# Value product of a hybrid attention trunk: the second read of one weight block is loaded with the first six tiles

## The chip, the cores and the metric

The kernel runs on one core of a Trainium2 chip. The metric is device time in microseconds of one execution. Three runs of the kernel before took 1443.1, 1443.45 and 1443.83 us (median 1443.45). One further execution was recorded by the hardware profiler and took 1444.35 us; all profile rows come from it, with times counted from the start of its span.

## The reference, cut to what matters

One layer over 1024 tokens of width 1024, in float32: an input projection gives queries, keys and values for 8 heads of a banded softmax attention (A) and 8 heads of a stick-breaking attention (B), and two gates; both branches are projected, gated, summed and projected again; LayerNorm, a SwiGLU feed-forward, LayerNorm.

```python
h = x @ w_in[l]
qa, ka, va, qb, kb, vb, ga, gb = jnp.split(h, split_pts, axis=-1)
y_a = chunk_band_attention(heads_a(qa), heads_a(ka), heads_a(va), rel_bias[l]) @ w_proj_a[l]
y_b = stick_breaking_attention(heads_b(qb), heads_b(kb), heads_b(vb)) @ w_proj_b[l]
mix = (sigmoid(ga + b_gate[l, :D]) * y_a + sigmoid(gb + b_gate[l, D:]) * y_b) @ w_out[l]
x = layer_norm(DEEPNORM_ALPHA * x + mix, ln1_g[l], ln1_b[l])
```

The change lies in the part of `x @ w_in` that gives `va` and `vb`: the value product, 1024 x 1024 times 1024 x 1024.

## The kernel before

**Arithmetic.** Every float32 operand is split into a high part, rounded on ScalarE (L110), and a low part, the difference, made on VectorE (L111); one product of a pair costs three matmuls (high by high, high by low, low by high). Large products are done by a seven-product scheme on 2 x 2 blocks (Strassen's, in Winograd's form): sums of blocks are formed on VectorE, seven block products p run in the order 1, 2, 6, 5, 7, 3, 4, and their results are added into four quarters. For the value product the weights are four blocks of 512 x 512, each held as two tiles of 128 x 1024 (halves h = 0, 1). X is block 0, U is block 3, Z is block 2, and block 1 is here called Y.

**Stages.** The input projection goes by pairs of column tiles: `plain` (pair 0), then pairs 1 to 4 (q and k), then the value product (`v`, `V_AT = 5`), pairs 6 to 8 (q and k) and five pairs of gates. Each pair has products named sxp, syp, szp; the tile `wcp4` is the third right operand of pair 4, read by its product 3 (szp<-s24h,wcp). Then come the attention heads one after the other (scores `sc_a`, transposes `tp_a`, value products `pv_a`, with gate matmuls `gps` mixed in as fill), the merge, and the FFN.

**The value product.** `v_load` (L413) runs while pair 4 computes; it asks for two tiles each of X, U and Z and issues their loads (L420). `v_prepare(p)` (L422) makes the operands of product p, while the product before it runs. For p = 1, 2, 5, 3, 4 it splits X, Z, X, U, Z as they stand at that time. For p = 6 it loads Y (L432) and forms, in place, X <- Y - X (L434), Y <- U - X (L435), Z <- Z - Y (L436), and splits the new Y. For p = 7 it loads block 1 again and takes U minus it (L438). High and low parts are `vh6`, `vl6` and so on, named by product. A product has 48 matmuls of 128 x 512 (2 halves, 4 rows of output j, 2 by 3 operands); products 1, 6, 7, 4 add up in one set of four PSUM banks, 2 in a second set, which 5 and 3 take over. After product 1 ScalarE copies the four banks out (`vc`, L489); after product 2 VectorE adds its banks on (L491), the sums are split and stored (L459).

**What sets the order.** All loads and stores go through SP's queue in the order in which the scheduler put them; a waiting one holds up those behind it. SBUF tiles come from rings of named buffers: `gt` has 3, `kp` 4, `op` 8; a new tile takes the buffer of the oldest tile of its tag and waits for that one's last reader. `cycle(QKV, ...)` goes round the four tags qs, kh, kl, v of two buffers each, so that eight tiles fill it once; stores of the pairs, outputs of the value product, gate tiles and later merged and FFN tiles all turn this ring, and the attention takes head tiles `qs`, `kh`, `kl`, `v` of the same buffers directly. The scheduler also decides the order on each engine from what it believes to be ready.

Of the kernel before, what the change touches and what calls it, by code (L numbers as in the profile page):

```python
# [48 lines left out]
def hybrid_trunk_kernel(ctx: ExitStack, tc, x, xt, w_first, w_v, w_in, b_gate, rel_bias, w_proj,  # L49
# [14 lines left out]
    def slot(tag, name, dtype=F32):  # L64
        return pool.tile([P, 1024], dtype, tag=tag, name=name, bufs=SLOTS[tag])
# [3 lines left out]
    def cycle(tags, name, dtype=F32):  # L69

        turn_of[tags] = turn_of.get(tags, -1) + 1
        return slot(tags[turn_of[tags] % len(tags)], name, dtype)

    QKV = ("qs", "kh", "kl", "v")
# [9 lines left out]
    dma = nc.sync.dma_start  # L84
# [24 lines left out]
    def split(dst_h, dst_l, src):  # L109
        return (nc.scalar.copy(dst_h, src),  # L110
                nc.vector.tensor_tensor(dst_l, src, dst_h.bitcast(F32), ALU.subtract))  # L111
# [298 lines left out]
    v_src = [[None] * 2 for _ in range(3)]  # L410
    v_ops = {}

    def v_load():  # L413

        for n, (blk, tags) in enumerate(((0, ("gt", "gt")), (3, ("gt", "kp")), (2, ("kp", "kp")))):
            for h, tag in enumerate(tags):
                v_src[n][h] = slot(tag, f"wv{blk}_{h}")
        for n, blk in ((0, 0), (2, 2), (1, 3)):
            for h in range(2):
                dma(v_src[n][h], w_v[blk, h])  # L420

    def v_prepare(p):  # L422

        put, sub = nc.vector.tensor_tensor, ALU.subtract
        v_ops[p] = []
        for h in range(2):
            X, U, Z = (v_src[n][h] for n in range(3))
            hi, lo = (slot("op", f"v{s}{p}_{h}", F32R) for s in "hl")
            src = {1: X, 2: Z, 5: X, 3: U, 4: Z}.get(p)
            if src is None:  # L430
                src = cycle(QKV, f"wv1_{p}{h}") if p == 6 else slot("gt", f"wv1_{p}{h}")
                dma(src, w_v[1, h])  # L432
                if p == 6:
                    put(X, src, X, sub)  # L434
                    put(src, U, X, sub)  # L435
                    put(Z, Z, src, sub)  # L436
                else:
                    put(src, U, src, sub)  # L438
            split(hi, lo, src)
            v_ops[p].append((hi, lo))  # L440

    def v_steps():
# [18 lines left out]
        def step(p, following):  # L461
# [3 lines left out]
            def run():  # L465
                if following:
                    v_prepare(following)
                if first:
                    for j in range(4):
                        tag = ("mm", "mm", "sc", "sc")[j] if accs is by else ("tr", "tr", "tr", "pv")[j]  # L470
                        accs[j] = bank(tag, f"v{p}_{j}")
                for h in range(2):
                    for j in range(4):
                        for i in range(2):
                            kt = 2 * h + i
                            xh_, xl_ = (x[:, j * P:(j + 1) * P] for x in ops_x[p][kt])
                            wh, wl = (w[:, (LO, HI)[i]] for w in v_ops[p][h])
                            for n, (a, b) in enumerate(((xh_, wh), (xh_, wl), (xl_, wh))):
                                mm(accs[j], a, b, start=(first and kt == n == 0),  # L479
                                   stop=(kt == 3 and n == 2), skip_group_check=True)  # L480
                for j in range(4):
                    acc = spread(accs[j])
                    if p == 4:
                        done("21", j, acc)
                        continue
                    name = {1: "11", 2: "11", 6: "12", 3: "12", 5: "22", 7: "22"}[p]
                    raw = tile_of(name, j)[1]
                    if p in (1, 6, 5):
                        nc.scalar.copy(raw, acc)  # L489
                    else:  # L490
                        nc.vector.tensor_tensor(raw, acc, raw, ALU.add)  # L491
                        done(name, j, raw)
# [134 lines left out]
    def right_or_v(i):  # L627
        if i + 1 == V_AT:
            v_load()
            v_prepare(1)  # L630
        else:
            right(i + 1)
# [794 lines left out]
```

## Time and profile before

| what | us |
|---|---|
| median of three runs | 1443.45 |
| profiled execution | 1444.35 |
| its span, first to last instruction | 1442.6 |
| busy: PE / VectorE / ScalarE / GpSimd | 1421.1 / 1028.6 / 673.0 / 267.8 |
| value product, first to last start on PE | 94.8 to 194.4 |
| attention heads | about 347 to 640 |

PE is the matmul engine, PEld its weight loads, DVE VectorE, ACT ScalarE, POOL GpSimd, SP the queue that issues the DMAs (SPq). A timeline row gives start, duration, engine, line, operation, out<-in, and in brackets the idle time of the engine before it with what ended it. A row of waits reads: who waited <- for whom: total, times, longest.

### The profile page before, as it was taken

How to read it: one execution, taken by the hardware profiler on the slowest of the kernel's cores; microseconds unless marked ns; L12 is line 12 of the kernel's file. 1: busy time of each engine (PE TensorE's matmuls, PEld its weight loads, DVE VectorE, ACT ScalarE, POOL GpSimd, SP SyncE). 2: the span in 40 equal slices, each digit the busy share in tenths (PEclk: the TensorE clock that was granted, in tenths of full speed). 3: DMA queues.
4: the chain of work that ended last, by engine and by line, in shares of the span. 5: the costliest groups of instructions: out<-in, count | busy, mean ns of one | idle time of the engine just before them, and what ended most of it. 6: DMA issues, size and time to landing. Idle time of an engine off the chain costs nothing.

```text
span 1442.6 us, 19078 instructions
## 1 busy us (share of the span) xinstructions
PE 1421.1 (99%) x6696; PEld 1178.6 (82%) x6696; DVE 1028.6 (71%) x1638; ACT 673.0 (47%) x1171; POOL 267.8 (19%) x317
## 2 busy tenths in 40 slices
PE   9997999999999999999999999999999999999997
PEld 7785888888888888888888888888888888888886
DVE  8856565654777878887858966676777755978757
ACT  6443444555787888773313634444444433221201
POOL 0000000001555778850014000000000000100016
PEclk9998999999999999999999999999999999999999
DMA  7565357868677587867512123434444457786602
GB/s 248 149 203 165 127 205 220 283 205 251 195 214 193 166 239 239 270 197 274 178 37 95 55 106 127 143 143 157 161 160 146 150 201 260 287 306 240 204 15 103
DMA packets 102544, 263.99 MB, mean 183 GB/s; under 512 B 11040, under 2 KB 27424, under 8 KB 102448
## 3 DMA queue, kind: packets, MB, share of 16 engines
q1 hardware_dynamic: 102448, 262.77, 55.5%
q8 instruction: 53, 0.87, 0.3%
q14 instruction: 43, 0.35, 0.1%
HBM read 170.94 MB, written 88.11 MB: 180 GB/s over the span
## 4 chain that ended last, share of the span: by engine, by line
PE 93%; DVE 3%; ACT 1%; DMA 1%; issue 1%; POOL 0%; SPq 0%; POOLq 0%; DVEq 0%; ACTq 0%
PE sxf L180 16%; PE sxp L180 8%; PE szf L180 8%; PE dx L1350 6%; PE v L479 5%; PE gps L573 4%; PE szp L180 4%; PE syf L180 4%; PE dz L1350 3%; PE yAps L870 3%; PE syp L180 2%; PE tp_b L781 2%; PE tp_a L781 2%; PE ops L118 2%; PE ops L117 2%; PE ops L120 2%
## 5 line engine op out<-in xcount | busy, mean ns | idle before, releaser
L1306 POOL TENSOR_TENSOR wdyt<-wdyt 128x512 f32<-128x512 f32 x8 | 11.1, 1394 | 512.3 <-ACT h L1178 422.6
L758 POOL TENSOR_TENSOR w_b<-w_b,kp_b 128x511 f32<-128x511 f32 (+3 forms) x96 | 96.4, 1015 | 31.8 <-DVE kp_b L753 22.5
L753 DVE TENSOR_TENSOR_SCAN kp_b<-kp_b,ident_ps 128x512 f32<-128x512 f32 (+2 forms) x64 | 56.6, 885 | 23.3 <-ACT kp_b L750 22.4
L750 ACT ACTIVATE kp_b<-sc_b 128x512 f32<-128x512 f32 (+3 forms) x96 | 48.4, 504 | 30.7 <-PE sc_b L670 25.4
L1058 POOL TENSOR_TENSOR mv<-mv,neghalf 128x1 f32<-128x1 f32 x16 | 23.9, 1494 | 207.6 <-DVE mv L1057 207.6
L693 POOL MEMSET bias<- 64x64 f32 x2 | 0.3, 145 | 327.3 <-ACT bias L689 327.3
L180 PE MATMUL szf<-x1S63h,wcf 128*128 128x512 f32 x168 | 55.1, 389 | 0.0
L111 DVE TENSOR_TENSOR pt_b<-tp_b,pt_b 128x512 fp32r<-128x512 f32 (+1 forms) x96 | 50.0, 544 | 6.8 <-ACT pt_b L110 6.2
L1281 DVE TENSOR_TENSOR x<-dx,x 128x512 f32<-128x512 f32 x64 | 43.5, 687 | 14.9 <-PE dx L1350 14.9
L723 POOL TENSOR_SCALAR w_a<-w_a,st_a 128x640 f32<-128x640 f32 (+2 forms) x64 | 42.4, 667 | 61.6 <-PE sc_a L670 26.5
L111 DVE TENSOR_TENSOR sl<-h,sl 128x512 fp32r<-128x512 f32 x56 | 38.5, 687 | 20.1 <-ACT sl L110 20.1
L110 ACT CAST sl<-h 128x512 fp32r<-128x512 f32 x56 | 34.7, 619 | 36.2 <-PE syf L180 17.1
L110 ACT CAST pt_b<-tp_b 128x512 fp32r<-128x512 f32 (+1 forms) x96 | 47.5, 505 | 8.0 <-PE tp_b L781 7.6
L718 ACT ACTIVATE w_a<-w_a,st_a 128x640 f32<-128x640 f32 (+2 forms) x64 | 44.8, 700 | 12.4 <-DVE st_a L712 11.2
L118 PE MATMUL ops<-wl_o,mh 128*128 128x512 f32 x128 | 50.1, 392 | 0.0
L120 PE MATMUL ops<-wh_o,ml 128*128 128x512 f32 x128 | 49.9, 390 | 0.0
L117 PE MATMUL ops<-wh_o,mh 128*128 128x512 f32 x128 | 49.7, 391 | 0.0
L1178 ACT ACTIVATE h<-sxf 128x512 f32<-128x512 f32 x21 | 12.6, 598 | 77.7 <-PE sxf L180 77.7
L751 ACT ACTIVATE w_b<-sc_b 128x511 f32<-128x511 f32 (+3 forms) x96 | 48.6, 506 | 0.0
L781 PE MATMUL tp_b<-ident,w_b 128*128 128x128 f32 x288 | 47.8, 273 | 0.4 <-DVE pt_b L111 0.3
L111 DVE TENSOR_TENSOR pt_a<-tp_a,pt_a 128x512 fp32r<-128x512 f32 (+1 forms) x96 | 44.8, 485 | 4.6 <-ACT pt_a L110 3.1
L110 ACT CAST pt_a<-tp_a 128x512 fp32r<-128x512 f32 (+1 forms) x96 | 39.1, 432 | 11.0 <-PE tp_a L781 10.7
(1740 smaller groups left out, 4784.8 us busy)
## 6 DMA issues: line engine op xcount, KB each, us to landing
s_dr<-sl SPq DMA_DIRECT2D x112, 256.0 KB, 2.3
sd<-s_dr SPq DMA_DIRECT2D x56, 512.0 KB, 4.8
wLf<-in_w_ffn_in_dram SPq DMA_DIRECT2D x22, 512.0 KB, 4.5
wRf<-in_w_ffn_in_dram SPq DMA_DIRECT2D x22, 512.0 KB, 3.5
v_dr<-vc SPq DMA_DIRECT2D x16, 512.0 KB, 3.0
kh<-k_dr SPq DMA_DIRECT2D x32, 256.0 KB, 5.8
kl<-k_dr SPq DMA_DIRECT2D x32, 256.0 KB, 6.0
qs<-q_dr SPq DMA_DIRECT2D x16, 512.0 KB, 5.5
```

The costliest lines, as they stand in the source:

```text
L110: return (nc.scalar.copy(dst_h, src), nc.vector.tensor_tensor(dst_l, src, dst_h.bitcast(F32), ALU.subtract))
L111: nc.vector.tensor_tensor(dst_l, src, dst_h.bitcast(F32), ALU.subtract))
L117: mm(acc, lh, rh, start=(i == 0), stop=False)
L118: mm(acc, lh, rl, start=False, stop=False)
L120: mm(acc, ll, rh, start=False, stop=(i == n))
L180: mm(acc, lw[:, ks], rx, start=(first and kt == i == 0), stop=(kt == 3 and i == 2), skip_group_check=not first)
L479: mm(accs[j], a, b, start=(first and kt == n == 0), stop=(kt == 3 and n == 2), skip_group_check=True)
L573: mm(acc[hf], lw[:, ks], rx[k][:, (LO, HI)[hf]], start=(k == j == 0), stop=(k == KT - 1 and j == 2))
L753: nc.vector.tensor_tensor_scan(kp[:, 0:e], kp[:, 0:e], ident_ps()[:, 0:e], 0.0, ALU.mult, ALU.add)
L758: nc.gpsimd.tensor_tensor(be[:, m0:e], be[:, m0:e], kp[:, m0 - 1:e - 1], ALU.mult)
L781: tr(tp[:, (qb - lo_q) * P:(qb - lo_q + 1) * P], wt[qb - q0][:, (kb - qb) * P:(kb - qb + 1) * P], ident)
L1350: mm(acc, a, b, start=(first and i == n == 0), stop=(i == n - 1 == 1), skip_group_check=not first)
```

## The change

Y's two tiles are asked for in `v_load`, one as the fourth `kp` tile, one from the QKV ring, and their loads are issued there, behind those of X, Z and U. `v_prepare(6)` takes these tiles; before, both were taken from the ring, and loaded, in `v_prepare(6)`. The second copy of block 1 for product 7 is loaded as before. Lines from L418 on move by up to four.

```diff
                 v_src[n][h] = slot(tag, f"wv{blk}_{h}")
+        again = [slot("kp", "wv1_60"), cycle(QKV, "wv1_61")]
         for n, blk in ((0, 0), (2, 2), (1, 3)):
             for h in range(2):
                 dma(v_src[n][h], w_v[blk, h])
+        for h in range(2):
+            dma(again[h], w_v[1, h])
+        v_src.append(again)
...
-            X, U, Z = (v_src[n][h] for n in range(3))
+            X, U, Z, Y = (v_src[n][h] for n in range(4))
             hi, lo = (slot("op", f"v{s}{p}_{h}", F32R) for s in "hl")
             src = {1: X, 2: Z, 5: X, 3: U, 4: Z}.get(p)
             if src is None:
-                src = cycle(QKV, f"wv1_{p}{h}") if p == 6 else slot("gt", f"wv1_{p}{h}")
-                dma(src, w_v[1, h])
+                src = Y if p == 6 else slot("gt", f"wv1_{p}{h}")
                 if p == 6:
                     put(X, src, X, sub)
                     put(src, U, X, sub)
                     put(Z, Z, src, sub)
                 else:
+                    dma(src, w_v[1, h])
                     put(src, U, src, sub)
```

The instructions are the same in number; their order moves. In SP's queue, in the value product (`wv2_1` and `wv3_1` are half 1 of Z and U, `wv1_60` and `wv1_61` the halves of Y, `k_dr4` and `q_dr4` the stores of pair 4, `vc11` the first output), before:

```order
L336 DMA q_dr4_81<-c1_4_959 64x1024
L432 DMA wv1_61_1155<-in_w_v_dram 128x1024
L459 DMA v_dr0_93<-vc11_0_1136 128x1024
L432 DMA wv1_60_1146<-in_w_v_dram 128x1024
L459 DMA v_dr0_93<-vc11_1_1138 128x1024
```

and now:

```order
L421 DMA wv2_1_966<-in_w_v_dram 128x1024
L421 DMA wv3_1_964<-in_w_v_dram 128x1024
L423 DMA wv1_60_967<-in_w_v_dram 128x1024
L423 DMA wv1_61_968<-in_w_v_dram 128x1024
L335 DMA k_dr4_89<-hi2_4_1053 64x1024
```

The two loads of Y moved ahead of the eight stores of pair 4 and of the stores of `vc11`; no other load changed its place there. On PE, product 3 of pair 4 (12 matmuls) moved from behind 4 matmuls of v to behind 22.

On VectorE, in product 2 (`wv0` X, `wv3` U, `wv2` Z), from the last work of pair 4 on, before:

```order
L389 SCALAR_TENSOR_TENSOR c1_4_959<-c1_4_959,hi1_4_1069 128x1024
L491 TENSOR_TENSOR vc11_0_1136<-v2_0_1162,vc11_0_1136 128x8x64
L491 TENSOR_TENSOR vc11_1_1138<-v2_1_1163,vc11_1_1138 128x8x64
L111 TENSOR_TENSOR vc11_0_1136<-vc11_0_1136 128x8x64
L491 TENSOR_TENSOR vc11_2_1140<-v2_2_1164,vc11_2_1140 128x8x64
L111 TENSOR_TENSOR vc11_1_1138<-vc11_1_1138 128x8x64
L491 TENSOR_TENSOR vc11_3_1142<-v2_3_1165,vc11_3_1142 128x8x64
L111 TENSOR_TENSOR vc11_2_1140<-vc11_2_1140 128x8x64
L111 TENSOR_TENSOR vc11_3_1142<-vc11_3_1142 128x8x64
L434 TENSOR_TENSOR wv0_1_962<-wv1_61_1155,wv0_1_962 128x1024
L435 TENSOR_TENSOR wv1_61_1155<-wv3_1_964,wv0_1_962 128x1024
L436 TENSOR_TENSOR wv2_1_966<-wv2_1_966,wv1_61_1155 128x1024
```

and now:

```order
L389 SCALAR_TENSOR_TENSOR c1_4_959<-c1_4_959,hi1_4_1073 128x1024
L437 TENSOR_TENSOR wv0_0_961<-wv1_60_967,wv0_0_961 128x1024
L438 TENSOR_TENSOR wv1_60_967<-wv3_0_963,wv0_0_961 128x1024
L437 TENSOR_TENSOR wv0_1_962<-wv1_61_968,wv0_1_962 128x1024
L439 TENSOR_TENSOR wv2_0_965<-wv2_0_965,wv1_60_967 128x1024
L111 TENSOR_TENSOR vl6_0_1149<-wv1_60_967,vh6_0_1148 128x1024
L438 TENSOR_TENSOR wv1_61_968<-wv3_1_964,wv0_1_962 128x1024
L495 TENSOR_TENSOR vc11_0_1140<-v2_0_1162,vc11_0_1140 128x8x64
L439 TENSOR_TENSOR wv2_1_966<-wv2_1_966,wv1_61_968 128x1024
L111 TENSOR_TENSOR vl6_1_1156<-wv1_61_968,vh6_1_1155 128x1024
L111 TENSOR_TENSOR vc11_0_1140<-vc11_0_1140 128x8x64
L495 TENSOR_TENSOR vc11_1_1142<-v2_1_1163,vc11_1_1142 128x8x64
```

The sums of Y stood behind all eight `vc11` instructions and now stand ahead of them, with one addition between. On ScalarE at the same place, now:

```order
L110 CAST vh6_0_1148<-wv1_60_967 128x1024
L110 CAST vh6_1_1155<-wv1_61_968 128x1024
L110 CAST vc11_0_1140<-vc11_0_1140 128x8x64
L110 CAST vh5_0_1230<-wv0_0_961 128x1024
L110 CAST vc11_1_1142<-vc11_1_1142 128x8x64
L110 CAST vh5_1_1234<-wv0_1_962 128x1024
L493 COPY vc11_3_1146<-v1_3_1091 128x8x64
```

Before, the copy of the fourth bank (`vc11_3<-v1_3`) stood ahead of the first cast of `vc11` and of all casts of `vh6`. On PE the product's fourth bank is now first written after 19 matmuls, the first product with half 1 one place ahead of it.

At the start of the attention, on SP (`qs1`, `kl1`, `v1` belong to head 1, `c1_13` and `c2_13` are the last gate tiles), before:

```order
L397 DMA g_dr8_111<-c1_13_2582 128x1024
L535 DMA wr_g11_2780<-in_w_in_dram 128x1024
L650 DMA qs1_2692<-q_dr0_77 128x1024
L663 DMA v1_2861<-v_dr0_93 128x8x128
L650 DMA qs2_2927<-q_dr1_78 128x1024
```

and now:

```order
L397 DMA g_dr8_111<-c1_13_2582 128x1024
L539 DMA wr_g11_2780<-in_w_in_dram 128x1024
L667 DMA v1_2861<-v_dr0_93 128x8x128
L657 DMA kl1_2697<-k_dr0_85 64x1024 x2
L654 DMA qs2_2927<-q_dr1_78 128x1024
```

Head 1's `kl` changed places with its `qs`, which now goes out earlier; a few of head 0's and head 1's matmuls on PE moved by some places with them. Behind the first three heads the order is again the same.

## The prediction

> **What bounds the kernel now.** I read the page first: the span and the engines' busy times.
>
> ```profile
> span 1442.6 us, 19078 instructions
> PE 1421.1 (99%) x6696; PEld 1178.6 (82%) x6696; DVE 1028.6 (71%) x1638; ACT 673.0 (47%) x1171; POOL 267.8 (19%) x317
> ```
>
> TensorE works 1421.1 of 1442.6 us. A change that adds and removes no matmul can win only where TensorE waits, or where its clock is cut. So the second view is the list of waits of PE, and the third the busy time and clock in stretches around the value product.
>
> ```profile
> PE v L479 <- ACT vh L110: 9.3, 1, 9.3
> PE warm L267 <- DVE warm L264: 1.2, 1, 1.2
> 120.00:130.00 10.00, 8.10 (x36) 6.38 (x34) 5.06 (x8) 2.48 (x4) 0.00 (x0) 1.00 0.77 203
> 130.00:140.00 10.00, 2.62 (x6) 1.94 (x7) 9.86 (x10) 3.72 (x4) 0.00 (x0) 0.65 0.48 190
> 140.00:150.00 10.00, 10.00 (x38) 8.04 (x38) 5.64 (x5) 2.40 (x4) 0.00 (x0) 0.84 0.32 105
> ```
>
> (After the stretch come its length and the busy times of PE, PEld, DVE, ACT, POOL, then the clock, DMA share and GB/s.) One wait of 9.3 us stands in the value product; the next in size is 1.2 us at the start. Around it the granted clock falls to 0.65 and 0.84, so the stall costs twice: idle, and then slow matmuls. The timeline of PE prices both.
>
> ```profile
> 127.71 0.39 PE L479 MATMUL v<-vh,xl 128*128 128x512 f32 x1
> 137.38 1.65 PE L479 MATMUL v<-vh,s24h 128*128 128x512 f32 x3 [9.28 <-ACT vh L110]
> ...
> 142.71 0.63 PE L479 MATMUL v<-vh,s24l 128*128 128x512 f32 x1
> 143.13 0.45 PE L479 MATMUL v<-vl,s24h 128*128 128x512 f32 x1
> ...
> 150.91 0.39 PE L479 MATMUL v<-vh,s24l 128*128 128x512 f32 x1
> 151.14 0.39 PE L479 MATMUL v<-vh,s13h 128*128 128x512 f32 x1
> ```
>
> A warm 128x512 matmul follows the one before after 0.227 us (150.91 to 151.14 is 0.23; product 5 runs like that throughout). Product 2 ends with the matmul at 127.71, so product 6 could start at 127.94; it starts at 137.38: 9.44 us. Its 48 matmuls last to 151.14, 13.76 us, where 48 x 0.227 is 10.88: 2.88 us more, all of it before 143.4, where starts lie 0.43 us apart. Together 12.32 us.
>
> What is late? Product 6 needs the tiles `vh6`, `vl6`, made by VectorE (L434 to L436) and ScalarE (L110) from Y, the block 1 that L432 loads.
>
> ```profile
> 120.31 0.62 SPq L336 DMA_DIRECT2D q_dr<-c  x1
> 121.04 1.01 SPq L432 DMA_DIRECT2D wv<-in_w_v_dram  x1
> 126.73 0.33 SPq L459 DMA_DIRECT2D v_dr<-vc  x1
> 127.18 0.37 SPq L432 DMA_DIRECT2D wv<-in_w_v_dram  x1
> DMA to landing us min/median/max: 3.5/4.6/5.7
> 117.92 1.22 DVE L389 SCALAR_TENSOR_TENSOR c<-c,hi 128x1024 f32<-128x1024 f32 x1
> 124.06 0.69 DVE L491 TENSOR_TENSOR vc<-v,vc 128x512 f32<-128x512 f32 x1 [4.92 <-PE v L479]
> 130.12 1.22 DVE L434 TENSOR_TENSOR wv<-wv,wv 128x1024 f32<-128x1024 f32 x1
> 131.37 1.23 DVE L435 TENSOR_TENSOR wv<-wv,wv 128x1024 f32<-128x1024 f32 x1
> 132.63 1.22 DVE L436 TENSOR_TENSOR wv<-wv,wv 128x1024 f32<-128x1024 f32 x1
> 133.77 1.22 DVE L434 TENSOR_TENSOR wv<-wv,wv 128x1024 f32<-128x1024 f32 x1
> 136.28 3.89 ACT L110 CAST vh<-wv 128x1024 fp32r<-128x1024 f32 x4 [6.81 <-DVE wv L435]
> ```
>
> Y is asked for in product 2 only: half 1 at 121.04, half 0 at 127.18, behind the first `vc` store, which waits for product 2's result. (`DMA to landing` is the time from issue to landing of all loads of block tiles, the group `wv`.) VectorE is idle for 4.92 us before 124.06, then clears the eight `vc` instructions and only then forms the six sums, 130.12 to 137.5. The first split ends at 137.3 and PE starts.
>
> **The change part by part.** It issues no instruction more or less: the two loads of Y move on SP from behind pair 4's stores to behind U's, and every tile of the QKV ring that follows takes a neighbouring buffer.
>
> *When Y lands.* On SP the six loads end so:
>
> ```profile
> 102.63 1.56 SPq L420 DMA_DIRECT2D wv<-in_w_v_dram  x2
> 113.19 0.45 SPq L335 DMA_DIRECT2D k_dr<-hi  x1
> 94.75 0.39 PE L479 MATMUL v<-vh,xh 128*128 128x512 f32 x1
> 95.66 0.43 PE L180 MATMUL szp<-s24h,wcp 128*128 128x512 f32 x1
> ```
>
> SP is free at 104.2. Y's half 0 takes the `kp` buffer of `wcp4`, which product 3 of pair 4 reads (szp<-s24h,wcp). Before, that starts at 95.66, after four matmuls of v; in the new order 22 stand ahead: 94.75 + 22 x 0.227 = 99.7, and with its own 12 it ends near 102.9. So no wait at 104.2; were there one, the queue behind holds pair 4's stores, which have nothing to send before 113.19: 9 us of cover. With 4.6 us (5.7 at most) to land, both halves are there by 110 to 111.
>
> *When product 6 is ready.* VectorE now takes the sums right behind L389 at 117.92. Starts lie 1.25 us apart where one reads the other's result (130.12, 131.37) and 1.14 where not (132.63, 133.77); a `vc` sum is 0.60. In the new order: X0 119.06, Y0 120.31, X1 121.45, Z0 122.59, vl6_0 123.73, Y1 124.87, vc_0 126.01 (its bank is ready, at 124.06 before), Z1 126.61, vl6_1 127.74, done 128.96. PE wants the first half at 127.94 and `vl6_1` after 25 matmuls, at 133.6: 3.0 us to spare on the first (vl6_0 is done at 124.95) and 4.6 us on the second. The 9.44 us go, and with them the idle time ahead of the slow matmuls, 2.88.
>
> *What is late next.* ScalarE's copy of the fourth bank out of product 1 (vc_3) has moved behind casts that follow VectorE's sums, and product 6 may not write that bank before it.
>
> ```profile
> 124.78 0.62 ACT L110 CAST vc<-vc 128x512 fp32r<-128x512 f32 x1 [6.11 <-DVE vc L491]
> 111.60 0.59 ACT L489 COPY vc<-v 128x512 f32<-128x512 f32 x1 [3.37 <-PE v L479]
> ```
>
> VectorE: low part of vc_0 at 128.88, sum vc_1 at 129.48, ended 130.17; ScalarE: cast vc_1 0.62, cast vh5_1 1.05, copy 0.59 with 0.1 overlap each, ending near 132.25. PE asks for the bank after 19 matmuls: 127.94 + 4.31 = 132.25. No slack. From below 0, from above one more 1.2 us VectorE instruction in the chain; I take 0.2, since every term is a measured one and the ends meet.
>
> *Products 5 and 7.* v5 is needed at 138.8 (127.94 + 10.88), its halves follow with five more instructions of VectorE each, near 132 and 135; v7's loads go out behind the last `vc` store, near 136, and land near 141: with one sum, one cast and one low part (1.23 + 1.05 + 1.22) near 145 for product 7 at 149.7. Nothing is taken for either.
>
> *The ring's turn.* Y now advances the ring once instead of twice, so every tile after the product sits one buffer further back. At the start of the attention one tile is worse off by it: head 1's `kl`. Its buffer is now that of a last gate tile, and its load stands on SP behind that tile's store and behind head 1's v.
>
> ```profile
> 345.18 2.94 SPq L397 DMA_DIRECT2D g_dr<-c  x2
> 348.69 0.73 SPq L650 DMA_DIRECT2D qs<-q_dr  x1
> 350.73 0.54 SPq L663 DMA_DIRECT2D v<-v_dr  x1
> 355.69 0.30 PE L670 MATMUL sc_a<-kl,qs 128*128 128x320 f32 x1
> 358.88 0.60 PE L781 MATMUL tp_a<-ident,w_a 128*128 128x128 f32 x4
> DMA to landing us min/median/max: 4.9/6.2/9.2
> ```
>
> (The last row is `kl` in 330 to 380 us.) On the clock of before, the second half of kl1 goes out at 351.9 and lands at 358.1, at worst 361.1. Its first reader was at 355.69. In the new order 7 gate, 4 value, 7 transpose matmuls and one of scores stand between the first scores with kh1 (near 355.3) and it: 12 x 0.227 or a little less, and 7 x 0.11 (four transposes take 0.60, the last one's 0.27 included), about 3.3 us, so near 358.6. Cost 0 to 2.5 us. The median landing leaves nothing, so I take a small 0.4.
>
> *Sum.* 12.3 - 0.2 - 0.4 = 11.7 us. The profiled execution took 1444.35 us (span 1442.6 and 1.75 around it): 1432.65. The median of the runs lies 0.9 below that execution, so **1431.8 us**.
>
> A rule on the slow matmuls: in the trace starts stay 0.43 us apart for 6.0 us after the stall (137.38 to 143.4), which cost 2.88. The Trainium skill (TensorE: Matmul & The Clock Gate, Part 1: The HAM clock gate) says that an idle window of some 3.4 us halves the clock and about 3.4 us of activity restores it; by that the slow matmuls cost half of 3.4, an estimate of 1.7 us, and the time would be 1433.0. The trace agrees on the half rate, not on the length; I go by the trace.
>
> **The rivals.** *(a) The attention pays more.* kl1 lands at its worst (2.5 us) and the copy of vc_3 at its upper bound (1.2 us): 12.3 - 3.7 = 8.6, so 1434.9. For it: the landings of `kl` there reach 9.2 us. Against: both ends at once. Chance 0.13.
>
> *(b) The wait moves to VectorE inside the product.* If the sums start late, by Y landing behind other loads or a sum waiting for a tile, PE waits again. It decides when the sums slip past their 3.0 us of slack at 119.06, so beyond 122. A slip by half of the old delay (6 of 11 us) leaves about 3 us idle and some slow matmuls, up to 2.9: gain 12.3 - 5.9 - 0.6, time 1437.7. For it: VectorE then has no pause from 117.9 to 135. Against: Y lands 8 us before it is wanted. Chance 0.07.
>
> ```profile
> PE tp_a L781 <- DVE pt_a L111: 0.4, 1, 0.4
> ```
>
> *(c) Slower: the turned ring.* All later users of the ring (projection stores, merged tiles, FFN operands, last weights) sit one buffer off; if two of them fall on buffers freed late on PE's path, each brings a landing, a cast and a low part, 4.6 + 1.05 + 1.22 = 6.9 us idle and 2.9 us of slow matmuls: 19.6 - 11.7 = 8 us slower, 1451. It wins from 12 us of new waits on. Against it: the row above is the longest wait of PE after the product, 0.4 us, and the order of instructions behind the attention's first heads is the same. Chance 0.04.
>
> *(d) It doesn't do what it says:* the sums wait for something else, such as U or the banks, and stay behind `vc`; 1443.4. But VectorE's new order has five of the six ahead of the `vc` work, and U and Z were read or landed by 109. Chance 0.02.
>
> **How the numbers follow.** Forecast 0.74, (a) 0.13, (b) 0.07, (c) 0.04, (d) 0.02. The forecast's own range is 1430.5 to 1433.2: neither of the small costs (1431.15) less the 0.7 us by which the runs of before differ (1443.1 to 1443.83), up to 1.4 us more than taken. To leave out no more than 2 in 10 the range takes (a) in, with 0.7 us of scatter: 1430.0 to 1435.6; at the low end 0.5 us more is allowed for, since matmuls in another order can also save. What can be told from no change is 0.2%, 2.9 us: faster needs under 1440.6, which the forecast, (a) and (b) are: 0.94; same 0.02; slower 0.04.
>
> **What would show it.** PE's list of waits has no `v` row over 1 us; the stretches 120 to 150 us show a clock of 1.00 and PE at 10.00; Y's two loads are issued near 104 and 105; VectorE's first sum starts near 119 and has no idle time before it; product 5 starts near 139, not 151. The copy of vc_3 ends near 132.3. In the attention the first reader of kl1 shows a wait of 0 to 2.4 us for its DMA. The forecast is wrong if a `v` wait of more than 1 us stays, or if a wait not listed above appears after 150 us.

## The result, and the profile after

The changed kernel takes 1432.29 us (median of four runs, 1432.19 to 1432.34); the kernel before took 1443.53 us in the four runs beside it (1443.1 to 1443.83). The ratio is 0.9922 with a 95% interval of 0.9905 to 0.9939. The forecast was 1431.8 us; the profiled execution took 1432.34 us against 1432.65 in the working.

The two longest waits of PE after (total, times, longest), and then the stretches around the value product:

```profile
PE warm L267 <- DVE warm L264: 1.2, 1, 1.2
PE tp_a L785 <- DVE pt_a L111: 0.4, 1, 0.4
```

```profile
120.00:130.00 10.00, 10.00 (x45) 8.26 (x44) 10.00 (x11) 3.82 (x5) 0.00 (x0) 1.00 0.30 75
130.00:140.00 10.00, 10.00 (x45) 8.04 (x44) 4.99 (x7) 5.30 (x9) 0.00 (x0) 1.00 0.81 293
140.00:150.00 10.00, 10.00 (x46) 8.29 (x45) 6.01 (x5) 5.48 (x7) 0.00 (x0) 1.00 0.54 175
```

The `v` row of 9.3 us is gone from the waits. PE is busy through all three stretches, and the granted clock, 0.65 and 0.84 before, is 1.00. Now VectorE is the full one from 120 to 130 us (10.00), as the sums have moved there. PE's timeline in the product:

```profile
127.28 0.39 PE L483 MATMUL v<-vh,xl 128*128 128x512 f32 x1
127.51 0.39 PE L483 MATMUL v<-vh,s24h 128*128 128x512 f32 x1
...
131.59 0.78 PE L483 MATMUL v<-vh,s24h 128*128 128x512 f32 x2
132.20 0.40 PE L483 MATMUL v<-vl,s24h 128*128 128x512 f32 x1
...
138.59 0.39 PE L483 MATMUL v<-vh,s13h 128*128 128x512 f32 x1
```

From the last matmul of product 2 (127.28) to the first of product 5 (138.59) pass 11.31 us, against 23.43 before (127.71 to 151.14). The 49 steps at 0.227 us would take 11.12, so 0.2 us of the 12.3 are still lost. Nearly all of that stands around 131.6: two matmuls and the next, from 131.59 to 132.20, take 0.61 where two steps are 0.45. What feeds this, in the timelines of SP, VectorE and ScalarE:

```profile
104.05 0.86 SPq L423 DMA_DIRECT2D wv<-in_w_v_dram  x2
118.63 1.22 DVE L437 TENSOR_TENSOR wv<-wv,wv 128x1024 f32<-128x1024 f32 x1
...
123.29 1.22 DVE L111 TENSOR_TENSOR vl<-wv,vh 128x1024 fp32r<-128x1024 f32 x1
...
127.30 1.22 DVE L111 TENSOR_TENSOR vl<-wv,vh 128x1024 fp32r<-128x1024 f32 x1
131.24 0.58 ACT L493 COPY vc<-v 128x512 f32<-128x512 f32 x1
```

Y's two loads go out from 104.05, the first sum starts at 118.63, `vl6_0` is done at 124.51 (3.0 us ahead of PE), `vl6_1` at 128.52 (wanted 25 matmuls after 127.51, at 133.2). The copy of the fourth bank ends at 131.82; PE wants the bank after 19 matmuls, at 127.51 + 19 x 0.227 = 131.82. That is the 0.2.

In the attention, the loads of `kl` for head 1 and their first reader on PE:

```profile
338.45 1.12 SPq L657 DMA_DIRECT2D kl<-k_dr  x2
346.08 0.55 PE L674 MATMUL sc_a<-kl,qs 128*128 128x320 f32 x2
```

The second half of `kl` is out by 339.6. In the stretch from 330 to 370 us a load of `kl` lands 5.1 to 7.5 us after its issue (median 6.9), and PE starts on `kl` at 346.08 with no idle time ahead of it. Still, a little is lost there. ScalarE's timeline of before, then of after, with the same two instructions:

```profile
339.02 0.59 ACT L212 COPY c<-szp 128x512 f32<-128x512 f32 x1 [2.13 <-PE szp L180]
400.63 0.62 ACT L718 ACTIVATE w_a<-w_a,st_a 128x384 f32<-128x384 f32 x1
```

```profile
326.47 0.59 ACT L212 COPY c<-szp 128x512 f32<-128x512 f32 x1 [2.13 <-PE szp L180]
388.27 0.62 ACT L722 ACTIVATE w_a<-w_a,st_a 128x384 f32<-128x384 f32 x1
```

Ahead of the attention the changed kernel is 12.55 us early (product 5: 151.14 - 138.59 = 12.55, too), behind its first heads 12.36. It is still 12.36 us early at ScalarE's last instruction (1420.17 against 1432.53), but 12.03 at the end of the span: behind that instruction the changed kernel takes 10.37 us, the kernel before 10.05. Two more profiles of before give 10.04 and 9.98, the kernels below from 9.76 (delay6) to 10.40 (delay2); what sets it stays open.

### The profile page after: what moved, and what is told of

Same layout as the page of the kernel before. It is cut to its first block, busy times and chain, and to the rows that moved or that the text cites. A ratio compares the mean times of both kernels' runs of the same rounds, so it can differ in the third digit from the quotient of the medians.

```text
span 1430.5 us, 19075 instructions
## 1 busy us (share of the span) xinstructions
PE 1418.6 (99%) x6696; PEld 1177.3 (82%) x6696; DVE 1027.6 (72%) x1638; ACT 672.9 (47%) x1171; POOL 267.8 (19%) x317
## 4 chain that ended last, share of the span: by engine, by line
PE 94%; DVE 3%; ACT 1%; issue 1%; POOL 0%; POOLq 0%; DVEq 0%; ACTq 0%
PE sxf L180 16%; PE sxp L180 8%; PE szf L180 8%; PE dx L1354 6%; PE v L483 5%; PE gps L577 4%; PE szp L180 4%; PE syf L180 4%; PE dz L1354 3%; PE yAps L874 3%; PE syp L180 2%; PE tp_b L785 2%; PE tp_a L785 2%; PE ops L117 2%; PE ops L118 2%; PE ops L120 2%
```

## The experiments

The slow matmuls are read in the same way for every kernel here: from the first matmul of product 6 to the first of product 5, less 48 x 0.227 = 10.88 us. Each kernel was compared with runs of the kernel before on the same chip; the medians of those were 1442.94 us for the first four kernels below, 1443.34 for delay2 and the three of the ring, and 1443.47 for delay4, delay6 and the two more profiles of before. The "page" with the 1.7 us or the window of 3.4 us in two of the expectations is that of the Trainium skill which the prediction names.

### The tiles of the change, loaded in the old place (late_tags)

```diff
-                src = cycle(QKV, f"wv1_{p}{h}") if p == 6 else slot("gt", f"wv1_{p}{h}")
+                src = (slot("kp", "wv1_60") if p == 6 and h == 0 else
+                       cycle(QKV, "wv1_61") if p == 6 else slot("gt", f"wv1_{p}{h}"))
```

(in the kernel before.) 

> The tiles of the change (one of the blocks' tag, one of the ring), but asked for and loaded where the kernel before does it. If the time of the loads decides: half 0 of Y no longer stands behind the first vc store, is loaded near 121 and landed by 126, but its sums still stand behind the vc work, at 130.1; two sums and a cast later, near 133.7, product 6 starts. PE waits 5.9 us in place of 9.4 and the slow matmuls stay: 1440. Rival, that the tags and the turned ring bring the gain and not the time of the loads: 1432.3.

Measured: 1441.15 us (10 runs, 1440.34 to 1442.39), ratio 0.9989 (0.9979 to 0.9998). SP, VectorE and PE:

```profile
120.37 1.04 SPq L433 DMA_DIRECT2D wv<-in_w_v_dram  x1
126.07 0.33 SPq L460 DMA_DIRECT2D v_dr<-vc  x1
129.45 1.22 DVE L435 TENSOR_TENSOR wv<-wv,wv 128x1024 f32<-128x1024 f32 x1
133.06 1.65 PE L480 MATMUL v<-vh,s24h 128*128 128x512 f32 x3 [5.63 <-ACT vh L110]
```

Half 0 goes out at 120.37, ahead of the first `vc` store, yet its sums start at 129.45 behind VectorE's `vc` work, and PE still idles 5.63 us. The tags alone bring a small part; the place of the loads brings the rest. The idle time is as expected. The median is 1.15 us above the expectation; by ScalarE's instructions, set beside those of the kernel before (before_again2), it is 4.1 us ahead behind the product, counted from the product's start, and 2.8 us at the end: 1.3 us are lost again in the attention and the FFN. What takes them is not known.

### One half of Y early (half0_early, half1_early)

```diff
-        again = [slot("kp", "wv1_60"), cycle(QKV, "wv1_61")]
+        again = [None, None]
+        again[0] = slot("kp", "wv1_60")
...
-        for h in range(2):
-            dma(again[h], w_v[1, h])
+        dma(again[0], w_v[1, 0])
...
                 if p == 6:
+                    if src is None:
+                        src = cycle(QKV, "wv1_61")
+                        dma(src, w_v[1, h])
                     put(X, src, X, sub)
```

For half 1 early, the early tile is the ring's and the late one is `wv1_60`, from the ring too.

> Only half 0 of Y is asked for and loaded early; half 1 comes from the ring in the old place, where it now stands behind the second vc store. If each half has to be there when product 6 reads it: product 6 starts without a wait, and stops after 24 matmuls for half 1: load near 128.6, landed near 133.4, two sums and a cast, 137.0 where PE asks near 133: 4.0 us idle, 0.5 more for the low part, and 0 to 2.9 of slow matmuls over the changed kernel: 1436.8 to 1439.7. Rival, that the first half alone held PE up: 1432.3.

> Only half 1 of Y is early; half 0 is loaded in the old place, now behind the third vc store, near 130, landed near 135. Two sums and a cast later, near 138.4, product 6 starts: 10.9 us idle, 1.4 more than before, with the slow matmuls: 1444 to 1445, slower than before although half of the change is in. Rival, that VectorE's length of work sets the start (three sums fewer in the way of it): 3 x 1.25 earlier than before, 1439.8.

Measured: half 0 early 1438.02 us (5 runs, 1437.6 to 1438.23; ratio 0.9965, 0.9952 to 0.9978); half 1 early 1444.12 us (10 runs, 1443.15 to 1445.54; ratio 1.0008, 0.9999 to 1.0017). Half 0 early, then half 1 early:

```profile
128.06 0.40 SPq L439 DMA_DIRECT2D wv<-in_w_v_dram  x1
133.17 1.23 DVE L440 TENSOR_TENSOR wv<-wv,wv 128x1024 f32<-128x1024 f32 x1 [3.43 <-DMA wv<-in_w_v_dram]
127.47 0.39 PE L486 MATMUL v<-vh,s24h 128*128 128x512 f32 x1
...
136.78 0.96 PE L486 MATMUL v<-vh,s24h 128*128 128x512 f32 x3 [3.71 <-ACT vh L110]
138.10 0.59 PE L486 MATMUL v<-vl,s24h 128*128 128x512 f32 x1 [0.36 <-DVE vl L111]
```

```profile
128.45 0.34 SPq L439 DMA_DIRECT2D wv<-in_w_v_dram  x1
133.47 1.23 DVE L440 TENSOR_TENSOR wv<-wv,wv 128x1024 f32<-128x1024 f32 x1 [3.62 <-DMA wv<-in_w_v_dram]
137.09 1.65 PE L486 MATMUL v<-vh,s24h 128*128 128x512 f32 x3 [9.96 <-ACT vh L110]
```

Both say the same: what counts is when each half is there. With half 0 early, product 6 starts at 127.47 without a wait and stops for half 1, 3.71 and 0.36 us (4.0 and 0.5 expected). With half 1 early, half 0 is issued behind three `vc` stores and VectorE itself waits for its landing (3.62 us); PE idles 9.96 us, 0.7 more than before, and nothing is gained. So the rival that a shorter list of VectorE work brings the start forward falls: in that run VectorE had idle time.

### The pause filled with matmuls (warm_fill)

```diff
+        next_by = []
...
+                if p == 6:
+                    next_by.append(bank("mm", "v5_0"))
+                    for n in range(38):
+                        mm(next_by[0], xh[0][:, 0:P], xh[0][:, LO], start=True, stop=True)
...
+                        if p == 5 and j == 0:
+                            accs[0] = next_by[0]
+                            continue
```

(in the kernel before; product 5 then overwrites that bank.) 

> The kernel before, with 38 matmuls of 128x512 without a use, between products 2 and 6, where PE waits (38 x 0.227 = 8.6 of the 9.4 us). Product 6 starts as late as before, near 137.4. If the idle time makes the matmuls behind it slow: they are at full rate now, and the time falls by the 2.9 us of the slow part, 1440.6; by the page's 1.7, 1441.8. If they are slow for another reason (the DMAs of that time, the operands arriving): no gain, 1443.5.

Measured: 1441.38 us (10 runs, 1441.15 to 1442.56), ratio 0.9990 (0.9980 to 0.9999).

```profile
127.38 8.78 PE L472 MATMUL v<-xh 128*128 128x512 f32 x38
136.83 1.20 PE L487 MATMUL v<-vh,s24h 128*128 128x512 f32 x4 [0.68 <-ACT vh L110]
...
148.27 0.39 PE L487 MATMUL v<-vh,s13h 128*128 128x512 f32 x1
```

Product 6 starts as late as before, at 136.83, and lasts 11.44 us to product 5 in place of 13.76; 48 steps would be 10.88. With 0.68 us of idle time in place of 9.3, the matmuls behind it are at full rate, but for 0.5 us in the first five steps (136.83 to 138.48), where PE also waits for the low part. So the idle time causes the slow matmuls; the DMAs and the operands were as late as ever. The gain is 1.56 us between medians. The one profile of before, 2.88, less the 0.56 that is left here, would give 2.3; the two profiles below give 1.6 and 1.8.

### The kernel before, profiled twice more (before_again1, before_again2)

> The kernel before, for another trace of its slow matmuls. If their number is fixed by the wait: again 14 at half rate over 6.0 us. If it varies from execution to execution: another length between 3.4 and 6.8, and a time that moves by half of the difference.

> As the run ahead of it: a third trace of the slow part of the kernel before, 6.0 us if it is fixed, another length with a time to match if it varies.

They took 1444.09 and 1442.80 us. PE in the first, then in the second:

```profile
127.40 0.39 PE L479 MATMUL v<-vh,xl 128*128 128x512 f32 x1
137.07 1.65 PE L479 MATMUL v<-vh,s24h 128*128 128x512 f32 x3 [9.28 <-ACT vh L110]
150.31 0.39 PE L479 MATMUL v<-vh,s13h 128*128 128x512 f32 x1
```

```profile
126.94 0.39 PE L479 MATMUL v<-vh,xl 128*128 128x512 f32 x1
136.61 1.65 PE L479 MATMUL v<-vh,s24h 128*128 128x512 f32 x3 [9.28 <-ACT vh L110]
...
141.00 0.39 PE L479 MATMUL v<-vh,s24h 128*128 128x512 f32 x1
...
149.61 0.39 PE L479 MATMUL v<-vh,s13h 128*128 128x512 f32 x1
```

The idle time is the same to the hundredth, 9.28 us; the slow part is not. It costs 13.24 - 10.88 = 2.36 and 13.00 - 10.88 = 2.12 us, where the first profile had 2.88. In the last of the three the full rate is back by 141.0, 4.4 us after the start, against 6.0 us. The other difference between these executions lies ahead of the product: it is reached 0.3 and 0.8 us earlier.

### VectorE later, step by step (delay2, delay4, delay6)

```diff
                     put(X, src, X, sub)
+                    if h == 0:
+                        for _ in range(4):
+                            put(X, X, X, ALU.max)
```

(in the changed kernel; 2, 4 and 6 times.) The scheduler sets sums of half 1 and `vc` work between the added instructions, so that half 0 is late by more than their own length: in delay4 its second sum starts at 128.42, 8.5 us behind that of the changed kernel (119.88), for 4.9 us added.

> The changed kernel with two more VectorE instructions of 1.22 us in half 0's chain, after its first sum (each takes the maximum of the tile with itself). Half 0's high part is then cast near 126.7, ahead of PE at 127.5, its low part done near 129.1, where PE asks at 128.2: 0.9 us of wait and no slow matmuls, 1433.2, if the slack of some 3 us is right. Rival, that VectorE's work from 117.9 to 135 is the bound already: all 2.4 us show, 1434.7.

> Four more VectorE instructions of 1.22 us in half 0's chain. Its high part is cast near 130.7, its low part done near 132.6: PE waits 3.2 us and then 1.0 us, 4.2 in all: 1436.5 if so short a wait leaves the clock alone, 1438 to 1439.4 with slow matmuls behind it. By the page's window of 3.4 us the wait is too short for a cut: 1436.5.

> Six more VectorE instructions in half 0's chain: high part near 134.3, low part near 136.2: PE waits 6.8 us and 1.0 us, and matmuls run at half rate behind it, 1.7 to 2.9 us: 1441.8 to 1443.0. If the clock cut came from the number of waits or from the DMAs and not from idle time: 1440.1.

Measured: 1433.58 us (4 runs, 1433.48 to 1434.19), 1437.78 (6 runs, 1436.99 to 1439.68) and 1441.14 (10 runs, 1440.42 to 1442.19). PE in the three, one after the other:

```profile
129.04 0.50 PE L486 MATMUL v<-vl,s24h 128*128 128x512 f32 x1 [0.76 <-DVE vl L111]
139.39 0.39 PE L486 MATMUL v<-vh,s13h 128*128 128x512 f32 x1
```

```profile
130.76 2.08 PE L486 MATMUL v<-vh,s24h 128*128 128x512 f32 x4 [3.12 <-ACT vh L110]
143.20 0.39 PE L486 MATMUL v<-vh,s13h 128*128 128x512 f32 x1
```

```profile
134.59 2.07 PE L486 MATMUL v<-vh,s24h 128*128 128x512 f32 x4 [6.59 <-ACT vh L110]
147.84 0.39 PE L486 MATMUL v<-vh,s13h 128*128 128x512 f32 x1
```

Two more instructions, 2.4 us of VectorE, cost PE 0.76 us of idle time (0.9 expected): the slack is there, and here it is just used up. With four and six PE idles 3.12 and 6.59 us (3.2 and 6.8 expected). Behind 3.12 us the matmuls are slow already, though one expectation had no cut behind so short a wait, and cost 12.44 - 10.88 = 1.56 us; behind 6.59 us 13.25 - 10.88 = 2.37. The short second wait for the low part, expected at 1.0 us, does not stand in the waits: at half rate the four matmuls ahead of it take long enough to cover it. The times: 1433.58 where 1433.2 was expected, 1437.78 just under the case with slow matmuls (1438 to 1439.4), and 1441.14, 0.7 us below the range, which had that second wait in it.

### The ring (after_again, ring_two, ring_phase)

```diff
-        again = [slot("kp", "wv1_60"), cycle(QKV, "wv1_61")]
+        again = [cycle(QKV, "wv1_60"), cycle(QKV, "wv1_61")]
```

is ring_two, and ring_phase turns the ring on by one more buffer:

```diff
         v_src.append(again)
+        turn_of[QKV] += 1
```

> The changed kernel once more, beside the next three on the same chip. 1432.3, and runs that differ by little: what made the runs of before differ is the slow part behind the long wait, which is gone.

> Both tiles of Y from the ring, asked for and loaded early; the ring then turns as far as before. If only the time of the loads counts and their buffers are free by 105: the product runs as in the changed kernel, and the attention gets back its 0.2 us: 1432.1 to 1432.3. Rival, that the tile from the blocks' tag is needed because the ring's buffers come free late: Y's load holds up pair 4's stores or lands behind 116, and PE waits some us in product 6: 1434 and more.

> The changed kernel, with the ring turned on by one more buffer after Y's tiles, so that all later tiles take the tags of the kernel before. If the turned ring costs something in the attention, 0.2 us by the profiles, it comes back: 1432.1; if those 0.2 us are chance: 1432.3. By the upper end of the prediction's term (2.5 us): 1430.

Measured on one chip, four runs each: the changed kernel 1432.18 us (1431.56 to 1432.38; ratio 0.9921, 0.9904 to 0.9937), ring_two 1431.75 (1431.61 to 1432.25; 0.9919, 0.9904 to 0.9934), ring_phase 1431.81 (1431.62 to 1432.92; 0.9921, 0.9906 to 0.9935). By the times the three are one. The changed kernel's four runs lie 0.82 us apart and ring_phase's 1.30, with no long wait of PE in the product in the one trace of each: the slow matmuls are not all that makes runs differ, as the expectation had it. The first matmul of product 5, one matmul behind the first heads (the same in each) and ScalarE's last instruction, in the changed kernel's second trace, in ring_two and in ring_phase:

```profile
138.38 0.39 PE L483 MATMUL v<-vh,s13h 128*128 128x512 f32 x1
382.61 0.28 PE L798 MATMUL pv_a<-pt_a,v 128*128 128x256 f32 x1
1419.94 1.15 ACT L1070 ACTIVATE x<-x,mv 128x1024 f32<-128x1024 f32 x1 [4.28 <-POOL mv L1062]
```

```profile
138.02 0.39 PE L483 MATMUL v<-vh,s13h 128*128 128x512 f32 x1
382.10 0.28 PE L798 MATMUL pv_a<-pt_a,v 128*128 128x256 f32 x1
1419.50 1.15 ACT L1070 ACTIVATE x<-x,mv 128x1024 f32<-128x1024 f32 x1 [4.29 <-POOL mv L1062]
```

```profile
138.02 0.39 PE L484 MATMUL v<-vh,s13h 128*128 128x512 f32 x1
382.12 0.28 PE L799 MATMUL pv_a<-pt_a,v 128*128 128x256 f32 x1
1419.77 1.15 ACT L1071 ACTIVATE x<-x,mv 128x1024 f32<-128x1024 f32 x1 [4.29 <-POOL mv L1063]
```

Both variants reach product 5 0.36 us earlier. Of that, 0.2 us is the wait for the fourth bank, which neither has (49 steps take 11.11 us in both), and the rest lies ahead of the product. From product 5 to the matmul in the middle pass 244.23 us in the changed kernel (244.27 in its first trace), 244.08 in ring_two and 244.10 in ring_phase. In the kernel before it stands at 395.26, 244.12 us behind product 5 (244.11 and 244.09 in two more profiles). PE's 292 matmuls ahead of it in the attention stand in the old order in both variants, and in another order at 36 places in the changed kernel. So the turned ring does cost some 0.15 us there, by the order of PE's work, and both variants get it back. ring_phase loses as much again right behind: by its last instruction only 0.17 of its 0.36 us are left. Where that goes is open, and it doesn't show in ring_two. And ring_two shows that the tile from the blocks' tag is not needed: asked for in time, both ring buffers are free as well (in its trace Y's loads go out at 103.52 and 103.99). Going by its trace ring_two is the best version here, by 0.4 us, which four runs can't tell from nothing.

## Why the prediction was right, and where it was off

**The idle time, 9.44 us.** Right: it is gone whole. That it hangs on the time at which the sums of each half can be made, once it has landed and VectorE's earlier work is out of the way (late_tags), and not on the tags or on the mere amount of VectorE's work, is shown by late_tags, half0_early and half1_early, whose waits of 5.63, 3.71 and 9.96 us were worked out ahead as 5.9, 4.0 and 10.9.

**The slow matmuls, 2.88 us.** Right in kind (warm_fill: no idle time, no slow matmuls) and right for the profiled execution. As a term for the median it was too large: three profiles of before gave 2.88, 2.36 and 2.12 us. The Trainium skill (TensorE: Matmul & The Clock Gate, Part 1: The HAM clock gate) says that the window runs free, so that the point of change moves by some 500 ns either way with where in it the work starts. The traces agree that it moves, but by more: behind equal idle times of 9.28 us the half rate lasted 6.0, 4.8 and 4.4 us. The estimate of 1.7 us in the prediction is near the low end of what was measured. Nor does the cost follow the length of the idle time: 1.56 us behind 3.12 (delay4), 1.73 behind 5.63 (late_tags, product 5 at 145.67), 2.37 behind 6.59 (delay6), 1.87 behind 9.96 (half1_early, product 5 at 149.84).

**The step that failed** is "the median of the runs lies 0.9 below that execution, so 1431.8". It carried the whole gap between one profiled execution and the median over to the changed kernel. By the three profiles of before, the gap has two parts. That execution's slow part was 0.4 us longer than the mean of the three (2.45), and this was taken away with the 2.88 already: it was counted twice. And it reached the end of product 2 late, at 127.71, against 127.40 and 126.94 in the two other traces and 127.28 in the changed kernel: these 0.4 us were rightly taken off. 1432.65 - 0.43 = 1432.22 is near the median (1432.29) and the profiled execution (1432.34); with the whole 0.9 taken off the forecast is 0.5 low. This rests on three executions and was not tested by itself. Some luck is in it, too: the attention cost 0.19 us where 0.4 was taken, and the 0.3 us at the end of the span had no term.

**The copy of vc_3, 0.2 us.** Right: no slack, with copy and request at the same 131.82. The size, between bounds of 0 and 1.2, was a choice and came out. **The ring's turn, 0.4 us.** Wrong in its mechanism: head 1's `kl` went out as foretold behind the gate tile's store, but was read at 346.08 without a wait. The turned ring cost some 0.15 us all the same, by PE's changed order at head 1, which ring_two and ring_phase do not have. What in that order costs the time is not shown.

**The slack of VectorE, 3.0 us**, and with it rival (b): the mechanism is real (delay2 to delay6), but 3.0 us of slack kept it away. Rivals (a), (c) and (d) did not come: no wait of PE behind the product is above 0.4 us.

## What to carry to other kernels

Where a wait sits at the end of the chain load, sums, cast, work out from the trace when each link could start, not when it did: here the load was late because its tile was asked for late, and everything else had room. Loading half of such an operand early can be worth much or nothing, according to which half is read first and which stores the other now stands behind. A wait of PE that cuts the clock costs a different amount in each execution; take the price from several profiles, and do not carry the gap between one profile and the median over to a kernel that no longer has the wait.

## What was not expected of the hardware

An idle time of 3.12 us was enough for matmuls at half rate behind it, at a cost of 1.56 us; 0.76 us was not. The cut need not show at once: in half0_early, behind 3.71 us, the first three matmuls started 0.34 us apart or less (136.78, 0.96 us for three), and the half rate came behind 138.10. Another wait, of 0.36 us, stands between.
